# State-space mixer of a hybrid encoder: the pooling product as one float32 matmul, rows read back on GpSimd's queue, and another order of the work

## The chip, the cores and the metric

The kernel runs on one core of a Trainium2 chip. The metric is the device time of one execution in microseconds (us), as the median of the runs of one version. A profile of one execution stands beside it. The engines are TensorE (PE, with its weight loads as PEld), VectorE (DVE), ScalarE (ACT), GpSimd (POOL) and SyncE (SP); SP, ACT and POOL also issue transfers, each on a queue of its own.

## What is computed

The reference is a trunk of two layers on 512 tokens of 1024 channels: a SwiGLU feed-forward part, a mixer, and a second feed-forward part in each. The change touches the mixer of the first layer, whose 1024 projected channels go half to a pooling mixer and half to a state-space mixer:

```
z  = hn @ ab_w_in
ya = pool_mixer(z[..., :512])      # 4 groups of 128 channels, windows 2, 4, 8, 16
yb = s5_mixer(z[..., 512:])        # 32 groups of 16 channels, 64 complex states each
m  = concatenate([ya, yb]) @ ab_w_out

# pool_mixer, group gi, window w:
p = windowed_mean(u, w) - u        # the mean over the tokens that lie inside the sequence
y = (p @ w_grp[gi]) * scale
# s5_mixer: s_t = lambda * s_(t-1) + B u_t, forward and backward; y = C s + D u
y = gelu(y);  y = y * sigmoid(y @ w_glu + b_glu)
```

## The kernel before

Most products are made from float32 operands as three matmuls on rounded parts (`mm3`, L179): each operand is a high part (`hi`, rounded on ACT) and a low part (`lo`, the rest, on DVE). Weights pass through the class `Weights` (`self.W`): `_load` issues a tile of 512 KB on SP's queue into one of two raw buffers, `hi` and `lo` (L117, L128) split it, `fill(n)` splits up to n tiles ahead of those in use, `take` hands out a split tile, `done` gives one back and by default fills again; a new load can't be issued before the low part of the tile in its raw buffer is made. Each engine and each queue works in the order of the program; an instruction that waits holds up what stands behind it on its engine or queue.

The mixer (L1373) begins with `first_proj` (L362), the projection of the four state-space tiles in two halves of the tokens; between the halves `start` allocates its tiles and issues the first loads. `chunk_rows` writes each projected tile to memory (`z_dram`, ACT's queue), and `u_rows` reads two tiles back, re-cut by chunk of tokens, into `us` (SP's queue). The state-space part then runs for four channel tiles `ct`: `inject` (float32 matmuls of `us` with a table `m` into the one tile `ps_x`), `decay` (a tile `rho` of decay factors on ACT), `scan` (on DVE: two products from `ps_x` with a table `e`, which release it, a sum and a difference, four recurrences, two products, four half-height sums; it is a generator that stops after the first two products and after the recurrences), `permute` (two copies of a table `i` on ACT), `output` (float32 matmuls with `us`, the states and a table `g` into `ps_y`, then a Gelu on ACT and a write to `y_dram` on ACT's queue), `y_rows` (read back, SP) and `split_y` (parts of y).

The pooling part runs for four channel tiles `i`: `pool_tile` (projection of 24 matmuls into `ps_p`, two copies `pz` and `pp` on ACT, window sums, edge factors and a difference on GpSimd; the returned `rest` splits the result into the tiles `yhl`, ACT and DVE), and `pool_out` (three matmuls with `w_pool`, then hi on ACT and lo on DVE, L399 and L400, into the tiles `xh`, `xl`, which the projection read before). `out_a` (L1553) multiplies tiles `kt` of the result with the output weights `w_ao` into `psA`; three of its four accumulators lie in the three banks `ps_A`, which `pool_out` uses as well. `glu` is the gate product; it begins after `output(3)`. The order of all of this is written out by hand in L1563 to L1640.

Of the kernel before, what the change touches and what calls it, by code (L numbers as in the profile page):

```python
# [15 lines left out]
P = 128  # L16
# [157 lines left out]
class Builder:  # L174
# [1198 lines left out]
    def mixer(self, nxt, before):  # L1373
# [20 lines left out]
        def start():  # L1394
            nonlocal yp, y, yhl, sp, us, edge
            yp = tc.alloc_tile_pool(name="mix_y", bufs=1)
            y = yp.tile([P, 4, SEQ], F32, name="y")
            yhl = [yp.tile([P, 4, SEQ], F32R, name=n) for n in ("y_hi", "y_lo")]
            sp = tc.alloc_tile_pool(name="mix", bufs=1)
            edge = sp.tile([P, 4, 16], F32, name="edge")  # L1400
            G.dma_start(edge, ins["pool_edge"].partition_broadcast(P))
            us = sp.tile([P, 32, 64], F32, name="us")
            load("m0", "e0")

        def chunk_rows(ct, ps):
# [5 lines left out]
            if ct == 2:  # L1411
                u_rows(0)

        def u_rows(ct):
            nc.sync.dma_start(us[:, 8 * ct:8 * ct + 16], self.by_chunk(self.z_dram[ct * P:(ct + 2) * P]))

        yp = y = yhl = sp = us = edge = None
        self.first_proj(4, "mix", before, start, chunk_rows)
        load("m1")
        u_rows(2)  # L1420
# [15 lines left out]
        def decay(ct):  # L1436
            rho = con[ct, "rho"] = sp.tile([P, 2, 4, 64], F32, tag="rho", bufs=2, name="rho")
# [65 lines left out]
        def split_y(ct):  # L1503
            hi, lo = (z[:, ct] for z in yhl)
# [3 lines left out]
        def pool_tile(i):  # L1508
# [23 lines left out]
            for k, (a, b) in enumerate(((0, win // 2), (SEQ - win // 2 + 1, SEQ))):  # L1532
                if b > a:
                    G.tensor_tensor(out=z[:, pad + a:pad + b], in0=z[:, pad + a:pad + b],
                                    in1=edge[:, i, 8 * k:8 * k + b - a], op=ALU.mult)
            G.tensor_tensor(out=p, in0=z[:, pad:pad + SEQ], in1=p, op=ALU.subtract)

            def rest():
                hl = [v[:, i] for v in yhl]
                nc.scalar.copy(hl[0], p)  # L1540
                V.tensor_tensor(out=hl[1], in0=p, in1=hl[0].bitcast(F32), op=ALU.subtract)

            return rest

        def pool_out(i):
            ps = self.bank("ps_A" if i < 3 else "ps_p")
            self.mm3(ps, [z[:, i * P:(i + 1) * P] for z in w_pool], [v[:, i] for v in yhl], True, True)
            self.split_evac(xh[:, i], xl[:, i], ps, scol[:, i:i + 1])

        lhs = lambda kt: (xh[:, kt], xl[:, kt])  # L1550
# [10 lines left out]
        for i, win in enumerate(self.POOL_W):  # L1561
            G.tensor_scalar(out=scol[:, i:i + 1], in0=scol[:, i:i + 1], scalar1=1.0 / win, scalar2=None, op0=ALU.mult)
        rest = [pool_tile(0)]  # L1563
        decay(0)
        decay(1)
        inject(0)
        load("g0")
        for _ in scan(0):
            pass
        rest.append(pool_tile(1))  # L1570
        rest[0]()
        decay(2)
        inject(1)
        load("m3", "e2")
        for _ in scan(1):
            pass
        rest.append(pool_tile(2))
        rest[1]()
        permute(0)
        decay(3)  # L1580
        inject(2)
        load("i1", "g1")
        self.W.done()
        output(0)
        turn = scan(2)
        next(turn)
        rest[2]()
        self.W.done()
        y_rows(0)
        load("e3", "g2")  # L1590
        for _ in turn:
            pass
        rest.append(pool_tile(3))
        permute(1)
        inject(3)
        output(1)
# [3 lines left out]
        w_pool = self.W.take()  # L1600
        for i in range(3):
            pool_out(i)
        turn = scan(3)
        next(turn)
        rest[3]()
        self.W.done()
        permute(2)
        out_a(range(3), range(2))
        next(turn)
        pool_out(3)  # L1610
        for _ in turn:
# [259 lines left out]
```

## Time and profile before

| | us |
|---|---|
| median of 3 runs | 1858.05 (1857.41 to 1858.77) |
| profiled execution, its own time | 1858.23 |
| its span, first to last instruction | 1856.5 |
| PE busy | 1796.5 |
| DVE busy | 1491.7 |
| ACT busy | 944.5 |
| POOL busy | 360.7 |

The mixer lies between 391 and 545 us of the span. A timeline row gives the start, the length, the engine, the line, the operation with output and inputs, the number of instructions merged into it, and in square brackets the idle time of the engine just ahead of it and what ended it. Matmuls overlap, so the pace of a run of them is read from start to start and not from their lengths. The granted clock (PEclk) is 1.00 at 2.4 GHz and 0.50 at 1.2 GHz.

### The profile page before, as it was taken

Reading aid. Unit: us, or ns where it says so; the run is one execution under the profiler, and the core shown is the slowest. Engines: PE = TensorE matmul, PEld = TensorE weight load, DVE = VectorE, ACT = ScalarE, POOL = GpSimd, SP = SyncE. Lnnn points to the kernel's source line nnn. Section 1 sums busy time; section 2 is a strip of 40 time slices with the busy share of each in tenths; the row PEclk is TensorE's granted clock in tenths of the full one; section 3 lists DMA queues with packets and bytes.
Section 4 is the critical chain, followed back from the end, with each engine's and each line's share of the span. In section 5 each row is a group of like instructions: output and inputs, shape, how many; then the busy total and the mean of one; then the engine's idle time right before and its main releaser. Section 6 shows DMA issues by size and latency. Waiting matters only on the chain.

```text
span 1856.5 us, 31301 instructions
## 1 busy us (share of the span) xinstructions
PE 1796.5 (97%) x12144; PEld 1623.3 (87%) x12144; DVE 1491.7 (80%) x2396; ACT 944.5 (51%) x1769; POOL 360.7 (19%) x254
## 2 busy tenths in 40 slices
PE   8999999998899999999999999999999999999998
PEld 7877997787679999988899998889888799999886
DVE  6898989968769999854899997456788689999745
ACT  6254456365455454444644545446777664454532
POOL 1021321014011323200123221001333013223100
PEclk9999999999999999999999999999999999999999
DMA  5474346637542333232233333223333223332331
GB/s 198 137 230 158 111 135 191 208 133 250 172 134 72 103 104 111 95 125 91 80 103 103 103 103 125 91 79 101 95 113 111 94 82 103 105 112 92 125 102 57
DMA packets 88931, 224.40 MB, mean 121 GB/s; under 512 B 16560, under 2 KB 29008, under 8 KB 87760
## 3 DMA queue, kind: packets, MB, share of 16 engines
q1 hardware_dynamic: 77088, 196.75, 32.5%
q0 software_dynamic: 6960, 23.57, 4.2%
q10 hardware_dynamic: 4736, 2.10, 0.4%
q8 instruction: 95, 1.56, 0.3%
q14 instruction: 52, 0.43, 0.1%
HBM read 205.64 MB, written 18.84 MB: 121 GB/s over the span
## 4 chain that ended last, share of the span: by engine, by line
PE 58%; DVE 9%; ACT 4%; issue 2%; DMA 1%; POOL 0%; DVEq 0%; ACTq 0%; POOLq 0%
PE ps_gu L183 10%; PE ps_gu L182 10%; PE ps_gu L181 10%; PE ps_A L181 3%; PE ps_A L183 3%; PE ps_A L182 3%; PE ps_B L183 3%; PE ps_B L182 3%; PE ps_B L181 3%; PE ps_f L181 2%; PE ps_f L183 2%; DVE w_lo L135 2%; PE ps_f L182 2%; ACT junk L237 1%; DVE xsum L518 1%
## 5 line engine op out<-in xcount | busy, mean ns | idle before, releaser
L135 DVE TENSOR_TENSOR w_lo<-w_raw,w_hi 128x1024 fp32r<-128x1024 f32 x214 | 283.0, 1327 | 210.7 <-ACT w_hi L124 208.0
L124 ACT CAST w_hi<-w_raw 128x1024 fp32r<-128x1024 f32 (+1 forms) x313 | 263.0, 864 | 280.3 <-PE ps_A L183 72.5
L183 PE MATMUL ps_gu<-xT_hi,w_lo 128*128 128x256 f32 (+1 forms) x1008 | 307.4, 305 | 2.5 <-DVE w_lo L135 2.5
L183 PE MATMUL ps_gu<-xsum,w_lo 128*128 128x256 f32 x1088 | 308.3, 283 | 0.8 <-DVE w_lo L135 0.8
L182 PE MATMUL ps_gu<-xsum,w_hi 128*128 128x256 f32 x1088 | 308.0, 283 | 0.2 <-DVE xsum L518 0.2
L181 PE MATMUL ps_gu<-xsum,w_hi 128*128 128x256 f32 x1088 | 307.7, 283 | 0.0
L181 PE MATMUL ps_gu<-xT_hi,w_hi 128*128 128x256 f32 (+1 forms) x1008 | 304.9, 302 | 0.0
L182 PE MATMUL ps_gu<-xT_lo,w_hi 128*128 128x256 f32 (+1 forms) x1008 | 304.6, 302 | 0.0
L183 PEld LDWEIGHTS ps_gu<-xsum,w_lo 128*128 128x128 f32 x1088 | 208.6, 192 | 1.0 <-DVE w_lo L135 0.9
L182 PEld LDWEIGHTS ps_gu<-xsum,w_hi 128*128 128x128 f32 x1088 | 208.5, 192 | 0.4 <-DVE xsum L518 0.4
L181 PEld LDWEIGHTS ps_gu<-xsum,w_hi 128*128 128x128 f32 x1088 | 208.4, 192 | 0.0
L183 PEld LDWEIGHTS ps_gu<-xT_hi,w_lo 128*128 128x128 f32 x1008 | 190.4, 189 | 14.8 <-DVE w_lo L135 3.9
L181 PEld LDWEIGHTS ps_gu<-xT_hi,w_hi 128*128 128x128 f32 x1008 | 190.3, 189 | 8.5 <-issue 0.9
L182 PEld LDWEIGHTS ps_gu<-xT_lo,w_hi 128*128 128x128 f32 x1008 | 190.2, 189 | 7.3
L109 POOL TENSOR_TENSOR w_u<-w_raw,w_s 128x512 f32<-128x512 f32 x64 | 112.1, 1751 | 355.2 <-ACT w_hi L124 196.1
L124 ACT CAST w_hi<-w_s 128x512 fp32r<-128x512 f32 x136 | 77.8, 622 | 197.4 <-DVE w_s L105 193.6
L135 POOL TENSOR_TENSOR w_lo<-w_raw,w_hi 128x1024 fp32r<-128x1024 f32 x31 | 74.2, 2394 | 494.9 <-ACT w_hi L124 471.2
L105 DVE TENSOR_TENSOR w_s<-w_raw,w_u 128x1024 f32<-128x1024 f32 x68 | 145.8, 2144 | 2.3
L640 POOL TENSOR_TENSOR g<-g,m 128x1024 f32<-128x1024 f32 x34 | 94.5, 2780 | 245.0 <-DVE m L638 245.0
L181 PE MATMUL ps_B<-w_hi,gT 128*128 128x512 f32 x352 | 137.1, 389 | 1.7 <-DVE free L1302 1.7
L183 PE MATMUL ps_A<-w_hi,gT 128*128 128x512 f32 x352 | 137.1, 389 | 1.1 <-DVE gT L693 1.1
L181 PE MATMUL ps_A<-w_hi,gT 128*128 128x512 f32 x352 | 137.3, 390 | 0.0
(381 smaller groups left out, 4229.5 us busy)
## 6 DMA issues: line engine op xcount, KB each, us to landing
w_raw<-in_w_gu_dram SPq DMA_DIRECT2D x106, 512.0 KB, 3.4
w_raw<-in_w_dn_dram SPq DMA_DIRECT2D x88, 512.0 KB, 3.3
w_u<-in_w_gu_dram SPq DMA_DIRECT2D x70, 512.0 KB, 3.8
w_raw<-in_w_qk_dram SPq DMA_DIRECT2D x16, 512.0 KB, 3.4
w_raw<-in_w_in_dram SPq DMA_DIRECT2D x8, 512.0 KB, 3.3
cm<-m_dram SPq DMA_DIRECT2D x4, 1024.0 KB, 9.3
w_raw<-in_w_ao_dram SPq DMA_DIRECT2D x8, 512.0 KB, 4.2
cg<-g_dram SPq DMA_DIRECT2D x4, 1024.0 KB, 8.0
```

The lines of the kernel that those rows point to most:

```text
L105: tt(out=blocks(s), in0=g[:, :HALF].unsqueeze(1).broadcast_to([P, 2, HALF]), in1=blocks(u)[:, :2], op=ALU.subtract)
L109: (h_engine or self.nc.gpsimd).tensor_tensor(out=z["h"], in0=g[:, HALF:], in1=z["s"][:, HALF:], op=ALU.add)
L124: self.nc.scalar.copy(hi[:, k:k + step], src[:, k:k + step])
L135: (engine or self.lo_engine).tensor_tensor(out=lo[:, :n], in0=src, in1=hi[:, :n].bitcast(F32), op=ALU.subtract)
L181: mm(ps, a[0], b[0], start=start, stop=False)
L182: mm(ps, a[0], b[1], start=False, stop=False)
L183: mm(ps, a[1], b[0], start=False, stop=stop)
L237: self.nc.scalar.activation(out=junk[:, :src.shape[-1]], in_=src, func=AF.Square, scale=scale, accum_out=out)
L518: tt(out=forms[n][1], in0=x, in1=forms[n][0].bitcast(F32), op=ALU.subtract)
L640: nc.gpsimd.tensor_tensor(out=rows(f), in0=rows(f), in1=m, op=ALU.mult)
```

## The change

The pool product becomes one float32 matmul on the unsplit result and unsplit weights; `w_pool` is no longer a tile of the weight list but is loaded by itself on GpSimd's queue (256 KB), so the splits of the four pooled results and of `w_pool` go. The results of the pool product go to the tiles `yhl`, under a new name, and no longer to `xh` and `xl`; the parts of y go to `xh` and `xl` in their place. So a pool product need not wait for the last pooling projection, and the four stand apart in the new order, each with its low part put off to a later point (`run_lows`). Each projected tile is read back into `us` on GpSimd's queue as soon as it is written, instead of two at a time on SP's. The load of `m1` moves into `start`. `rho` has one buffer instead of two. The edge factors of both ends are applied in one instruction, and the scales are multiplied in one. The order of the mixer's work is written anew: `inject` and `pool_tile` change places, `decay` stands beside its own scan, and the splits of the two `w_ao` tiles stand behind scan 1 and behind scan 2. The diff, without the constants of the edge table and the weight list, from which `w_pool` is taken out:

```diff
@@ -1392,15 +1392,17 @@
                                   src if kind == "e" else src.rearrange("p u x -> p (u x)"))
 
         def start():
-            nonlocal yp, y, yhl, sp, us, edge
+            nonlocal yp, y, yhl, sp, us, edge, w_pool
             yp = tc.alloc_tile_pool(name="mix_y", bufs=1)
             y = yp.tile([P, 4, SEQ], F32, name="y")
-            yhl = [yp.tile([P, 4, SEQ], F32R, name=n) for n in ("y_hi", "y_lo")]
+            yhl = [yp.tile([P, 4, SEQ], F32R, name=n) for n in ("pool_hi", "pool_lo")]
             sp = tc.alloc_tile_pool(name="mix", bufs=1)
-            edge = sp.tile([P, 4, 16], F32, name="edge")
+            edge = sp.tile([P, 4, 17], F32, name="edge")
             G.dma_start(edge, ins["pool_edge"].partition_broadcast(P))
+            w_pool = sp.tile([P, HALF], F32, name="w_pool")
+            G.dma_start(w_pool, ins["w_pool"])
             us = sp.tile([P, 32, 64], F32, name="us")
-            load("m0", "e0")
+            load("m0", "e0", "m1")
 
         def chunk_rows(ct, ps):
 
@@ -1408,16 +1410,10 @@
             nc.scalar.copy(zt, ps)
             rows = self.z_dram[ct * P:(ct + 1) * P]
             nc.scalar.dma_start(rows, zt)
-            if ct == 2:
-                u_rows(0)
-
-        def u_rows(ct):
-            nc.sync.dma_start(us[:, 8 * ct:8 * ct + 16], self.by_chunk(self.z_dram[ct * P:(ct + 2) * P]))
-
-        yp = y = yhl = sp = us = edge = None
+            G.dma_start(us[:, 8 * ct:8 * ct + 8], self.by_chunk(rows))
+
+        yp = y = yhl = sp = us = edge = w_pool = None
         self.first_proj(4, "mix", before, start, chunk_rows)
-        load("m1")
-        u_rows(2)
         load("m2", "e1", "i0")
         self.new_psum(ps_x=(1, 1024), ps_y=2, ps_p=1, ps_A=3)
 
@@ -1434,7 +1430,7 @@
                                              us[:, 8 * ct + 2 * n + a, :], start=True, stop=True)
 
         def decay(ct):
-            rho = con[ct, "rho"] = sp.tile([P, 2, 4, 64], F32, tag="rho", bufs=2, name="rho")
+            rho = con[ct, "rho"] = sp.tile([P, 2, 4, 64], F32, tag="rho", bufs=1, name="rho")
             for d in range(2):
                 col = 16 * d + 4 * ct
                 nc.scalar.copy(rho[:, d], self.rho8[:, col:col + 4].unsqueeze(2).broadcast_to([P, 4, 64]))
@@ -1501,7 +1497,7 @@
             nc.sync.dma_start(y[:, ct], self.y_dram[ct * P:(ct + 1) * P])
 
         def split_y(ct):
-            hi, lo = (z[:, ct] for z in yhl)
+            hi, lo = xh[:, ct], xl[:, ct]
             nc.scalar.copy(hi, y[:, ct])
             V.tensor_tensor(out=lo, in0=y[:, ct], in1=hi.bitcast(F32), op=ALU.subtract)
 
@@ -1529,25 +1525,18 @@
                     G.tensor_tensor(out=s[:, o + h:e - h], in0=z[:, o:e - 2 * h], in1=z[:, o + 2 * h:e], op=ALU.add)
                     o, e = o + h, e - h
                 z, s = s, z
-            for k, (a, b) in enumerate(((0, win // 2), (SEQ - win // 2 + 1, SEQ))):
-                if b > a:
-                    G.tensor_tensor(out=z[:, pad + a:pad + b], in0=z[:, pad + a:pad + b],
-                                    in1=edge[:, i, 8 * k:8 * k + b - a], op=ALU.mult)
+            ends = z[:, pad:pad + SEQ].rearrange("p (a n) -> p a n", n=8)[:, 0:64:63]
+            G.tensor_tensor(out=ends, in0=ends, in1=edge[:, i, :16].rearrange("p (a n) -> p a n", n=8), op=ALU.mult)
             G.tensor_tensor(out=p, in0=z[:, pad:pad + SEQ], in1=p, op=ALU.subtract)
-
-            def rest():
-                hl = [v[:, i] for v in yhl]
-                nc.scalar.copy(hl[0], p)
-                V.tensor_tensor(out=hl[1], in0=p, in1=hl[0].bitcast(F32), op=ALU.subtract)
-
-            return rest
-
-        def pool_out(i):
+            pooled.append(p)
+
+        def pool_out(i, later):
+
             ps = self.bank("ps_A" if i < 3 else "ps_p")
-            self.mm3(ps, [z[:, i * P:(i + 1) * P] for z in w_pool], [v[:, i] for v in yhl], True, True)
-            self.split_evac(xh[:, i], xl[:, i], ps, scol[:, i:i + 1])
-
-        lhs = lambda kt: (xh[:, kt], xl[:, kt])
+            nc.tensor.matmul(ps, w_pool[:, i * P:(i + 1) * P], pooled[i], start=True, stop=True)
+            self.split_evac(*(x[:, i] for x in yhl), ps, scol[:, i:i + 1], later)
+
+        lhs = lambda kt: [x[:, kt] for x in (yhl if kt < 4 else (xh, xl))]
         psA, wA = [None] * TT, []
 
         def out_a(ts, kts):
@@ -1558,65 +1547,73 @@
                     psA[t] = self.bank("ps_A" if t < 3 else "ps_y")
                 self.rows(psA[t], lhs, kt, t, wA[kt // 2], kt % 2, kt == 0, kt == KT - 1)
 
-        for i, win in enumerate(self.POOL_W):
-            G.tensor_scalar(out=scol[:, i:i + 1], in0=scol[:, i:i + 1], scalar1=1.0 / win, scalar2=None, op0=ALU.mult)
-        rest = [pool_tile(0)]
+        pooled, lows = [], []
+
+        def run_lows():
+            while lows:
+                lows.pop(0)()
+
+        G.tensor_tensor(out=scol, in0=scol, in1=edge[:, :, 16], op=ALU.mult)
         decay(0)
-        decay(1)
         inject(0)
+        pool_tile(0)
         load("g0")
         for _ in scan(0):
             pass
-        rest.append(pool_tile(1))
-        rest[0]()
+        decay(1)
+        inject(1)
+        pool_tile(1)
+        load("m3", "e2")
+        turn = scan(1)
+        next(turn)
+        permute(0)
+        inject(2)
+        pool_out(0, lows)
+        for _ in turn:
+            pass
+        run_lows()
+        self.W.done(2, fill=False)
+        self.W.fill(3)
         decay(2)
-        inject(1)
-        load("m3", "e2")
-        for _ in scan(1):
-            pass
-        rest.append(pool_tile(2))
-        rest[1]()
-        permute(0)
-        decay(3)
-        inject(2)
         load("i1", "g1")
-        self.W.done()
+        pool_tile(2)
         output(0)
+        y_rows(0)
+        load("e3", "g2")
         turn = scan(2)
         next(turn)
-        rest[2]()
-        self.W.done()
-        y_rows(0)
-        load("e3", "g2")
+        inject(3)
+        pool_out(1, lows)
+        pool_tile(3)
+        self.W.done(2, fill=False)
+        permute(1)
+        output(1)
         for _ in turn:
             pass
-        rest.append(pool_tile(3))
-        permute(1)
-        inject(3)
-        output(1)
+        run_lows()
+        self.W.fill(2)
+        decay(3)
         load("i2")
         y_rows(1)
         load("g3", "i3")
-        w_pool = self.W.take()
-        for i in range(3):
-            pool_out(i)
+        pool_out(2, lows)
+        out_a(range(3), range(2))
         turn = scan(3)
         next(turn)
-        rest[3]()
-        self.W.done()
+        run_lows()
         permute(2)
-        out_a(range(3), range(2))
+        pool_out(3, lows)
+        output(2)
         next(turn)
-        pool_out(3)
+        run_lows()
+        out_a(range(3), range(2, 4))
         for _ in turn:
             pass
-        output(2)
         permute(3)
         split_y(0)
         split_y(1)
-        out_a(range(3), range(2, 4))
         y_rows(2)
-        self.W.done(2)
+        self.W.fill(4)
         output(3)
         y_rows(3)
         wide = self.bank("ps_x")
...
```

## Rows read from the trace of the kernel before

**Rows 1.** The page: busy time of each engine, share of the span, instructions.

```profile
PE 1796.5 (97%) x12144; PEld 1623.3 (87%) x12144; DVE 1491.7 (80%) x2396; ACT 944.5 (51%) x1769; POOL 360.7 (19%) x254
```

**Rows 2.** Windows: length, busy time by engine, granted clock, DMA share, GB/s.

```profile
424.00:475.00 51.00, 36.57 (x535) 30.73 (x534) 47.54 (x50) 26.67 (x43) 22.95 (x27) 0.93 0.74 249
475.00:505.00 30.00, 29.94 (x288) 24.14 (x287) 20.73 (x26) 12.36 (x16) 0.00 (x0) 0.95 0.54 167
```

**Rows 3.** Timeline of TensorE in the mixer.

```profile
426.87 0.50 PE L181 MATMUL ps_p<-xT_hi,w_hi 128*128 128x512 f32 x1
...
432.66 2.09 PE L1432 MATMUL ps_x<-us,cm 128*64 128x64 f32 x64
...
444.01 3.53 PE L1432 MATMUL ps_x<-us,cm 128*64 128x64 f32 x64 [3.19 <-issue]
...
459.39 2.09 PE L1432 MATMUL ps_x<-us,cm 128*64 128x64 f32 x64 [3.25 <-issue]
461.28 0.32 PE L1489 MATMUL ps_y<-us,perm 128*64 128x64 f32 x4
...
474.23 0.80 PE L181 MATMUL ps_A<-w_hi,xT_hi 128*128 128x512 f32 x1 [7.66 <-DVE xT_lo L400]
...
478.12 0.39 PE L181 MATMUL ps_A<-w_hi,xT_hi 128*128 128x512 f32 x1
...
483.94 0.50 PE L181 MATMUL ps_A<-w_hi,xT_hi 128*128 128x512 f32 x1
...
488.33 0.34 PE L1489 MATMUL ps_y<-us,perm 128*64 128x64 f32 x4
...
491.52 0.50 PE L181 MATMUL ps_x<-y_hi,w_hi 128*128 128x512 f32 x1
```

**Rows 4.** Timeline of VectorE in the mixer.

```profile
422.00 1.22 DVE L135 TENSOR_TENSOR w_lo<-w_raw,w_hi 128x1024 fp32r<-128x1024 f32 x1 [1.62 <-ACT w_hi L124]
426.79 1.22 DVE L1450 TENSOR_TENSOR t<-ps_x,ce 128x1024 f32<-128x1024 f32 x1 [3.57 <-PE ps_x L1432]
...
436.30 4.62 DVE L1467 TENSOR_TENSOR s<-t,t 64x512 f32<-64x512 f32 x4
...
475.40 1.21 DVE L1450 TENSOR_TENSOR t<-ps_x,ce 128x1024 f32<-128x1024 f32 x1
...
486.18 2.81 DVE L1467 TENSOR_TENSOR s<-t,t 64x512 f32<-64x512 f32 x4
```

**Rows 5.** The tile pp's instructions: count, ns min/median/max, first and last start.

```profile
L1541 DVE TENSOR_TENSOR y_lo<-pp,y_hi x4: 682/694/1008, 440.9 to 477.7; 128x512 fp32r<-128x512 f32 x4
```

**Rows 6.** Timeline of ScalarE in the mixer (ACTq is its transfers).

```profile
411.21 0.35 ACTq L1410 DMA_DIRECT2D z_dram<-zt  x1
...
420.92 1.05 ACT L124 CAST w_hi<-w_raw 128x1024 fp32r<-128x1024 f32 x1 [1.16 <-DMA w_raw<-in_w_in_dram]
...
456.17 1.09 ACT L1519 COPY pz<-ps_p 128x512 f32<-128x512 f32 x1 [0.26 <-PE ps_p L183]
...
457.98 2.10 ACT L1476 COPY perm<-ci 128x512 f32<-128x512 f32 x2
464.37 0.60 ACT L1496 ACTIVATE yt<-ps_y 128x512 f32<-128x512 f32 x1 [4.29 <-PE ps_y L1493]
```

**Rows 7.** Transfers, KB, us to landing (unnamed row: reads into us); last: GpSimd issues.

```profile
z_dram<-zt ACTq DMA_DIRECT2D x1, 256.0 KB, 3.2
...
DMA to landing us min/median/max: 5.9/7.6/9.2
...
ci<-i_dram SPq DMA_DIRECT2D x1, 512.0 KB, 4.1
...
g_dram<-ssm_tab POOLq DMA_DIRECT2D x10, 256.0 KB, 3.5
...
L1284 POOL DMA_DIRECT2D g_dram<-ssm_tab x10 | 7.6, 769 | 27.9 <-ACT ssm_tab L1279 27.9
```

**Rows 8.** Windows, columns as in rows 2: the stretch behind the 3.19 us stand.

```profile
444.00:446.00 2.00, 1.99 (x38) 2.00 (x40) 2.00 (x2) 1.35 (x2) 1.84 (x3) 0.50 0.37 150
```

More of the change, by code (lines that the diff above doesn't have):

```diff
@@ L1630, in glu @@
                 self.mm3(psG[d], [z[:, kt % 2 * HALF + d * P:kt % 2 * HALF + (d + 1) * P] for z in wG[kt // 2]],
-                         [z[:, kt] for z in yhl], kt == 0, kt == 3)
+                         [z[:, kt] for z in (xh, xl)], kt == 0, kt == 3)
         glu(range(3), range(2))
@@ L1684, in mid_weights @@
         if ly == 0:
-            l = [w["w_in"][i] for i in (4, 5, 6, 7, 0, 1, 2, 3)] + [w["w_pool"]]
+            l = [w["w_in"][i] for i in (4, 5, 6, 7, 0, 1, 2, 3)]
             l += [w["w_ao"][0, i] for i in range(2)] + [w["w_glu"][i] for i in range(2)]
@@ L1816, in lay_out @@
     bias = bias.reshape(16, 4, P, 256).transpose(0, 2, 1, 3)
-    edge = np.zeros((4, 16), np.float32)
+    edge = np.ones((4, 17), np.float32)
     for i, w in enumerate(Builder.POOL_W):
         edge[i, :w // 2] = [w / (t + w // 2) for t in range(w // 2)]
-        edge[i, 8:7 + w // 2] = [w / (w - 1 - k) for k in range(w // 2 - 1)]
+        edge[i, 17 - w // 2:16] = [w / (w - 1 - k) for k in range(w // 2 - 1)]
+        edge[i, 16] = 1 / w
     lanes = lambda z: z.reshape(2, 16, 2, 64, -1).transpose(2, 3, 0, 1, 4).reshape(P, 32, -1)
@@ L1838, in lay_out @@
         "w_in": col_tiles(a["ab_w_in"][0]),
-        "w_pool": np.concatenate([a["pool_w"][0].transpose(1, 0, 2).reshape(P, HALF),
-                                  np.zeros((P, HALF), np.float32)], axis=1),
+        "w_pool": a["pool_w"][0].transpose(1, 0, 2).reshape(P, HALF),
         "w_glu": a["ssm_w_glu"][0].reshape(2, 2, P, HALF).transpose(0, 2, 1, 3).reshape(2, P, 1024),
```

## The prediction

> **What bounds the kernel now.** I read the shares of busy time first: TensorE (PE) is busy 97% of the span [rows 1], so nothing can be won where PE never waits. The busy times by stretch then show where it does wait: from 424 to 475 us, inside the state-space mixer, PE is busy 36.57 of 51 us and VectorE (DVE) 47.54, while from 475 to 505 PE is busy 29.94 of 30 [rows 2]. The change works in just that first stretch. PE's own order of work shows the three stands: 3.19 us before inject(2), 3.25 before inject(3), 7.66 before the output product out_a [rows 3]. The first two wait for a scan's first two products (L1450, L1451), which release the one `ps_x` tile; the third waits for the low part of a pooled result (L400), which stands on DVE behind scan 2. So DVE's queue is the pace: from its first scan product at 426.79, which sat idle 3.57 us before, to the end of scan 3 at 486.18+2.81 = 488.99 [rows 4]. PE then ends output(3) and begins the gate product at 491.52 [rows 3]. Behind that point the code is unchanged, so I compare the start of the gate product, and every microsecond there counts as one in the total. The profiled execution took 1858.23 (span 1856.5 and 1.7 around it), the median of the runs 1858.05; I apply the difference to the median.
>
> **Work that goes.** Four splits of pooled results: on DVE 0.69, once 1.01, in sum 3.1 us [rows 5], and as many copies on ScalarE (ACT). One weight split (`w_pool`): about 1.2 on DVE and 1.05 on ACT [rows 4, 6]. With GpSimd out of the way the pieces overlap a little, so DVE's queue gets some 3.9 us shorter. GpSimd does four edge products instead of seven and one scaling instead of four; it only has to be done by the time a pool product wants its tile, and that is later than its work in all of what follows.
>
> **The product.** Three rounded matmuls of about 0.23 (18 of them take 488.33-483.94 = 4.4) make 0.70; the float32 one is not in the trace at 512 columns. inject is float32: 32 matmuls of 64 columns in 2.09 us [rows 3]. If the two 64-wide halves run one after the other, 512 columns cost 8 x 2.09/32 = 0.52; if side by side, 1.04. I take 0.9, nearer the second, since the halves use different columns of the array. Four of them: between -0.7 and +1.4 us of PE, I take +0.8, of which only the last stands on the path below (+0.2, bounds -0.2 and +0.3). The Trainium skill (FP8 and Floating Point Precision, TensorE Precision Notes) says that true float32 makes four passes, which speaks against the change, as an estimate 4/3 of 0.70 = 0.93 and the same sum within 0.1.
>
> **The start.** Scan 0 needs inject(0), and that the rows `us` of its chunk. Before, a pair of chunks came back on SyncE's queue; now each one on GpSimd's. The first row write is issued at 411.21 [rows 6] and landed 3.2 later; a GpSimd issue of this kind takes 0.77, and 256 KB on its queue landed in 3.5, while the `us` reads took 5.9 to 9.2 [rows 7]. So us(0) lands between 418.7 and 424.4; I take 420.3, near the first, since it has half the bytes. inject(0) adds 2.0 (459.39 to 461.28 [rows 3]): 422.3. But DVE first has the low part of the fourth `w_in` tile, which ended at 422.00+1.22 = 423.2, and its ACT half had waited 1.16 for the load [rows 4, 6]. Now `m1`, 1 MB, stands ahead of that load: at 249 GB/s [rows 2] at most 4.2 us, at least 0; it is issued when the second half of the projection begins, long before, so I take 1.2, near the lower end. Scan 0 begins at 424.4 (423.2 to 427.4), 2.4 us sooner. PE stands about 1.3 us at 419 and does pool_tile(0) later; the cover is its wait at inject(2), which stays.
>
> **The new order, step by step.** Between 426.79 and 488.99 DVE has four scans and, beside them, 3.1 of pool splits, 3.7 of three weight splits and 2.8 of pooled low parts: (62.2-9.6)/4 = 13.2 us a scan. Scans 0 and 1: 424.4+26.4 = 450.8. Low part of product 0 and the first `w_ao` split: 0.7+1.2, 452.7. First two products of scan 2: 2.4, 455.1; now `ps_x` is free. PE: inject(3) 2.0, product 1 0.9, pool_tile(3) 5.8 (426.87 to 432.66): 463.8. ACT: the copies `pz` and `pp` 1.8 (456.17 to 457.98) and the first of permute(1) 1.05: 466.7. output(1) to its Gelu 3.1 (461.28 to 464.37): 469.8. Gelu 0.6 and the issue of its write 0.35 [rows 6]: 470.8. Here is the new wait: the high part of the second `w_ao` tile stands behind this Gelu on ACT (`fill(2)` after output(1)), 1.05, 471.8, and DVE had finished scan 2 and product 1's low part at 455.1+10.8+0.7 = 466.6. It stands 5.2 us, which is most of the 6.3 (2.4+3.9) it had won. Behind that wait are queued on DVE the low part (1.2, 473.0), scan 3's first two products (2.4, 475.4) and the low part of product 2 (0.7, 476.1). For that last one PE waits: out_a's third token tile wants the third `ps_A` bank, which product 2 holds. PE's own work reached this at 469.8+0.9+1.5 = 472.2, so it stands 3.9 us. Then 12 of out_a's 18 matmuls 2.9, product 3 0.9, output(2) 3.0, the second out_a 4.4, output(3) with its end 3.2 (488.33 to 491.52): 490.5. That is 1.0 sooner than 491.5.
>
> **What lies beside.** `i2` is queued on SyncE behind the load that waits for that second low part: 473.0+0.4, landing 4.1 later [rows 7], 477.5; permute(2) ends at 479.6, product 3's high part at 480.5, its low part on DVE at 481.2, and scan 3's last part takes 5.2 (two products as long as its first two, 2.4, and sums of 2.81 [rows 4]): 486.4, inside PE's 487.3. `e3` stands behind y_rows(0), which waits for output(0)'s write. inject(2) waits for scan 1's first two products (437.6+2.4 = 440.0); with 3.5 for it as before, a product 0.9, pool_tile(2) 5.8, output(0) 3.1 and the Gelu the write is issued near 454.3: even with 9.2 for the write and for `e3` [rows 7] it lands at 472.7, as scan 3 begins. One `rho` buffer makes ACT wait for each scan's recurrences; behind them are queued the pool copies, which PE delivers later anyway.
>
> **The clock.** After the stand of 7.66 us the first nine matmuls took from 474.23 to 478.12, 3.9 us where nine of 0.23 are 2.1: 1.8 lost. After 3.19 us the granted clock was 0.50 (the 1.2 GHz level) and inject took 3.53; after 3.25 us it took 2.09 as ever [rows 3, 8]. The new stand of 3.9 us lies between: half of 1.8, +0.9. Sum: -1.0+0.9 = -0.1, 1858.1 against 1858.23, and 1858.0 by the median.
>
> **The rivals.** *Scans run free, faster.* Scan 3, beside an idle GpSimd, took 488.99-475.40 less 2.4 for others = 11.2, and four half-height sums beside GpSimd's adds took 4.62 instead of 2.81 [rows 4]. If the new order keeps GpSimd's adds away from scans 0 and 1 (2.0 each) and the start loses nothing to `m1` (1.2), all of the chain is 5.2 sooner: 1852.8. For it: DVE is the pace up to scan 2. Against: the same adds run, and two pool tiles still fall in those scans. By the Trainium skill (SBUF - State Buffer, Who interferes with whom) only VectorE instructions with two SBUF inputs contend with GpSimd's reads; the slow sums agree, and products with one PSUM input go free. By that, pool_tile(1)'s adds beside scan 1's first products would cost about 1 us less, 1857.0. Chance 0.27 for more than 3.7 us sooner.
>
> *A crowded start, slower.* `m1`, `w_pool`, the row writes and the small pieces of `us` on a third queue share the DMA engines; if all of `m1` (4.2) delays us(0) and its read takes 9.2, it lands at 414.4+4.2+0.8+9.2 = 428.6, scan 0 begins at 430.8, 6.4 later than I say: 1864.4. It decides from a scan start of 424.4 on, one for one, and is slower by over 0.2% from 428.2. Against: GpSimd's own queue landed such sizes in 3.5. Chance 0.15.
>
> *The edit doesn't act as read.* The third bank comes free otherwise, or the product costs 0.52: output(2) is then held by permute(2)'s first copy, 478.6, and the end is 1.3 sooner still, 0.9 more without the cold clock: 1855.8. That lies within 0.2%, with the forecast: together 0.58.
>
> **How the numbers follow.** 0.2% is 3.7 us, about what a measurement of this kernel can tell from no change. Faster 0.27, same 0.58, slower 0.15. The likeliest case alone reaches from 1854.3 to 1861.7. The range goes down to the free scans and up to the middle of the crowded start: 1852.5 to 1862.5.
>
> **What would show it.** Right: scan 0's first product near 424.4; DVE idle some 5 us before the second `w_ao` low part, released by ACT; PE idle some 4 us in out_a, released by L400; the stand of 7.66 gone; the gate product near 490 to 491.5. Wrong: DVE busy without a break up to scan 3 (then the gate product comes near 485), scan 0 after 427, or a wait for `e3` or `i2` that sets scan 3.

## The result: slower by 0.8%, and the profile after

The changed kernel takes 1873.62 us at the median (1868.87 to 1879.24), the kernel before 1858.77 beside it: a ratio of 1.0079 (1.0065 to 1.0094). The forecast was 1858.0 with a range up to 1862.5, so it was wrong, and on the side to which it gave a chance of 0.15. The profiled execution took 1873.31, 15.1 more than that of before.

The page, as [rows 1], and the windows, as [rows 2]. PE waits less than before in the first stretch (40.20 busy of 51, before 36.57), though part of that busy time is a lower granted clock (0.87, before 0.93), and more in the second (26.01 of 30, before 29.94), where it had no idle time to lose; the granted clock falls there from 0.95 to 0.83.

```profile
PE 1802.2 (96%) x12140; PEld 1626.1 (87%) x12140; DVE 1485.5 (79%) x2391; ACT 941.3 (50%) x1764; POOL 362.3 (19%) x253
...
424.00:475.00 51.00, 40.20 (x454) 32.96 (x454) 43.69 (x46) 18.38 (x30) 18.42 (x25) 0.87 0.61 215
475.00:505.00 30.00, 26.01 (x337) 20.99 (x338) 17.42 (x22) 13.95 (x20) 4.38 (x5) 0.83 0.40 128
```

TensorE's timeline, as [rows 3]: the stands are the numbers in brackets, with what ended them. inject(0) and inject(3) now follow stands of 4.65 and 6.08 us, output(1) one of 3.06. The last one, 3.61, lies behind the gate product, where no code was changed.

```profile
424.67 3.68 PE L1428 MATMUL ps_x<-us,cm 128*64 128x64 f32 x64 [4.65 <-issue]
...
461.85 3.41 PE L1428 MATMUL ps_x<-us,cm 128*64 128x64 f32 x64 [6.08 <-issue]
465.18 1.13 PE L1536 MATMUL ps_A<-pp,w_pool 128*128 128x512 f32 x2
465.74 0.80 PE L181 MATMUL ps_p<-xT_hi,w_hi 128*128 128x512 f32 x1
...
474.96 0.45 PE L1485 MATMUL ps_y<-us,perm 128*64 128x64 f32 x4 [3.06 <-ACT perm L1472]
...
485.96 0.80 PE L181 MATMUL ps_A<-w_hi,pool_hi 128*128 128x512 f32 x1 [3.99 <-DVE pool_lo L400]
...
491.25 1.45 PE L1536 MATMUL ps_p<-pp,w_pool 128*128 128x512 f32 x2
...
502.92 0.50 PE L181 MATMUL ps_x<-xT_hi,w_hi 128*128 128x512 f32 x1
...
532.93 0.39 PE L183 MATMUL ps_B<-w_hi,pool_lo 128*128 128x512 f32 x1
536.92 0.80 PE L181 MATMUL ps_B<-w_hi,pool_hi 128*128 128x512 f32 x1 [3.61 <-ACT junk L237]
```

VectorE's timeline, as [rows 4]: scan 0 begins at 428.39; in scan 1 the recurrences (L1455) take 4.39 and the four sums (L1463) 4.38, in scan 2 they take 2.43 and 2.79; then DVE stands 10.14 us for the high part of the second `w_ao` tile.

```profile
428.39 1.22 DVE L1446 TENSOR_TENSOR t<-ps_x,ce 128x1024 f32<-128x1024 f32 x1 [3.10 <-PE ps_x L1428]
...
441.63 1.23 DVE L1446 TENSOR_TENSOR t<-ps_x,ce 128x1024 f32<-128x1024 f32 x1
...
446.14 4.39 DVE L1455 TENSOR_TENSOR_SCAN t<-rho,t 128x256 f32<-128x256 f32 x4
...
453.08 4.38 DVE L1463 TENSOR_TENSOR s<-t,t 64x512 f32<-64x512 f32 x4
...
462.99 2.43 DVE L1455 TENSOR_TENSOR_SCAN t<-rho,t 128x256 f32<-128x256 f32 x4
...
468.05 2.79 DVE L1463 TENSOR_TENSOR s<-t,t 64x512 f32<-64x512 f32 x4
...
481.76 1.23 DVE L135 TENSOR_TENSOR w_lo<-w_raw,w_hi 128x1024 fp32r<-128x1024 f32 x1 [10.14 <-ACT w_hi L124]
```

GpSimd's additions for pool_tile(1) and pool_tile(2) both begin inside scan 1:

```profile
445.75 1.42 POOL L1525 TENSOR_TENSOR pz<-pz 128x541 f32<-128x541 f32 x1
...
455.49 2.90 POOL L1525 TENSOR_TENSOR pz<-pz 128x541 f32<-128x541 f32 x2
```

ScalarE's timeline, as [rows 6], says why VectorE stands those 10.14 us: the high part `w_hi` stands behind the Gelu of output(1), that behind permute(1), that behind the copies `pz` and `pp` of pool_tile(3).

```profile
471.99 1.07 ACT L1515 COPY pz<-ps_p 128x512 f32<-128x512 f32 x1 [4.96 <-PE ps_p L183]
472.86 1.13 ACT L1516 ACTIVATE pp<-ps_p 128x512 f32<-128x512 f32 x1
473.77 2.07 ACT L1472 COPY perm<-ci 128x512 f32<-128x512 f32 x2
479.63 0.60 ACT L1492 ACTIVATE yt<-ps_y 128x512 f32<-128x512 f32 x1 [3.78 <-PE ps_y L1489]
480.26 0.38 ACTq L1493 DMA_DIRECT2D y_dram<-yt  x1
480.68 1.05 ACT L124 CAST w_hi<-w_raw 128x1024 fp32r<-128x1024 f32 x1 [0.45 <-ACT yt L1492]
```

Transfers issued in one microsecond each (KB, us to landing), as [rows 7]: `m1` needs 10.4 us, and the first row write, issued behind it at 411.78, 8.2 where it was 3.2; the first read of `us`, issued at 420.25, needs 4.3 more.

```profile
cm<-m_dram SPq DMA_DIRECT2D x1, 1024.0 KB, 10.4
...
z_dram<-zt ACTq DMA_DIRECT2D x1, 256.0 KB, 8.2
...
us<-z_dram POOLq DMA_DIRECT2D x1, 256.0 KB, 4.3
```

### The profile page after: what moved, and what is told of

Same layout as the page of the kernel before. It is cut to its first block, busy times and chain, and to the rows that moved or that the text cites. A ratio compares the mean times of both kernels' runs of the same rounds, so it can differ in the third digit from the quotient of the medians.

```text
span 1871.5 us, 31290 instructions
## 1 busy us (share of the span) xinstructions
PE 1802.2 (96%) x12140; PEld 1626.1 (87%) x12140; DVE 1485.5 (79%) x2391; ACT 941.3 (50%) x1764; POOL 362.3 (19%) x253
## 3 DMA queue, kind: packets, MB, share of 16 engines
q8 instruction: 95, 1.56, 0.4%
## 4 chain that ended last, share of the span: by engine, by line
PE 64%; DVE 17%; ACT 6%; DMA 6%; issue 4%; POOL 1%; SPq 1%; DVEq 0%; ACTq 0%; POOLq 0%
PE ps_gu L183 11%; PE ps_gu L182 11%; PE ps_gu L181 11%; DVE w_lo L135 3%; PE ps_A L181 3%; PE ps_A L182 3%; PE ps_A L183 3%; PE ps_B L181 3%; PE ps_B L182 3%; PE ps_B L183 3%; DMA w_raw<-in_w_gu_dram 2%; ACT w_hi L124 2%; PE ps_f L183 2%; PE ps_f L181 2%; PE ps_f L182 2%
```

## The experiments

The code ahead of the mixer is the same in all kernels, yet `m0`'s load is issued between 404.68 and 410.07 us of the span in their profiled executions. So beside the median of the timed runs the table has the traces' times counted from that issue (start of the named instruction, for scans 1 and 3 the end of the last sum, for the column "end" the end of the span). Each of those times is of one execution. The kernel before, run again beside each group of experiments, took 1857.92 to 1859.28 at the median.

| kernel | scan 0 | scan 1 ends | inject(3) | scan 3 begins | scan 3 ends | gate product | second tile of ps_B | end | median, us |
|---|---|---|---|---|---|---|---|---|---|
| before | 19.78 | 48.15 | 52.38 | 68.39 | 81.97 | 84.50 | 115.05 | 1449.4 | 1858.77 |
| changed | 20.81 | 49.87 | 54.26 | 75.32 | 91.93 | 95.33 | 129.34 | 1464.0 | 1873.62 |
| e2_m1_late | 18.37 | 46.45 | 50.85 | 72.81 | 88.05 | 91.46 | 125.36 | 1460.4 | 1867.34 |
| e3_hi_early | 20.68 | 48.69 | 53.09 | 64.04 | 84.92 | 88.31 | 122.27 | 1457.0 | 1867.27 |
| e5_bank_order | 20.51 | 49.57 | 53.96 | 74.81 | 91.24 | 94.64 | 125.25 | 1458.5 | 1870.15 |
| e6_three | 18.04 | 45.03 | 49.83 | 62.53 | 82.51 | 85.92 | 116.13 | 1448.9 | 1857.12 |
| e7_three_perm | 17.29 | 45.08 | 49.36 | 63.05 | 78.41 | 81.83 | 112.17 | 1445.3 | 1854.23 |
| e8_us_sp | 22.72 | 50.15 | 54.54 | 75.44 | 91.88 | 95.29 | 129.24 | 1463.1 | 1871.25 |
| e10_before_f32b | 20.10 | 48.45 | 52.07 | 67.65 | 80.70 | 84.05 | 114.38 | 1445.9 | 1856.84 |
| e12_perm_us_sp | 20.15 | 49.15 | 53.54 | 64.35 | 81.48 | 84.90 | 115.15 | 1448.7 | 1859.47 |
| e13_no_adds | 20.51 | 45.41 | 49.69 | 69.43 | 86.03 | 89.45 | 123.42 | 1457.3 | 1866.94 |
| e14_before_no_adds | 20.09 | 45.60 | 49.83 | 63.01 | 76.58 | 79.11 | 109.35 | 1442.4 | 1852.04 |
| e15_warm | 19.07 | 46.90 | 52.04 | 71.60 | 88.07 | 91.47 | 121.72 | 1455.5 | 1863.63 |

My theory was three separate losses: a crowded start, the place of one ScalarE instruction, and one PSUM bank. The rivals stand in each expectation.

**The start.** e2 puts `m1` back behind the first projection.

```
-            load("m0", "e0", "m1")
+            load("m0", "e0")
...
-        load("m2", "e1", "i0")
+        load("m1", "m2", "e1", "i0")
```

> The changed kernel with m1 loaded behind the first projection again, as in the kernel before; the small reads of us stay on GpSimd's queue and w_pool stays early. Theory (crowded start): without this 1 MB the first row write lands 3 to 5 us after its issue instead of 8.2, us(0) is there near 420.5, scan 0 starts near 424.5 instead of 428.4, and the cold stand before inject(0) is gone: 3 to 5 us less, about 1869.6. Rival (the reads on GpSimd's queue or w_pool are what is slow): us(0) still lands near 424 and the time stays at 1873.6.

The first row write, issued at 408.88, landed in 4.3 us instead of 8.2, scan 0 began 2.4 us sooner by the table, the end came 3.6 sooner, the median fell by 6.3. (The two profiled executions differ by 6.5, of which 2.9 lie ahead of `m0`, so the table's 3.6 is the better measure; 1.0 of it is a shorter scan 1.) So `m1` was in the way, as the rival "crowded start" had it.

```profile
z_dram<-zt ACTq DMA_DIRECT2D x1, 256.0 KB, 4.3
```

e4 makes the same edit the other way round, in the kernel before: `load("m0", "e0", "m1")`, and no `load("m1")` behind.

> The kernel before with one edit of the change, m1 loaded with m0 ahead of the second half of the first projection. Theory (crowded start): its row writes land late as in the changed kernel, scan 0 starts 2 to 4 us later than 426.8, the time rises by 2 to 4 us, to about 1861.5. Rival (the crowd comes from w_pool or from the small reads): no change, 1858.8.

It took 1857.91, no change: here the rival held. The first row write did land late (6.8 us), but a pair of chunks waits for the second write anyway, and that landed at 420.02 instead of 418.43; inject(0) began 0.3 us later, counted from `m0`. So an early `m1` costs only the one who reads each chunk as soon as it is written: it takes back what the single reads should win. e8 undoes those in the changed kernel, where `m1` stays early:

```
-            G.dma_start(us[:, 8 * ct:8 * ct + 8], self.by_chunk(rows))
+            if ct % 2:
+                ct -= 1
+                nc.sync.dma_start(us[:, 8 * ct:8 * ct + 16], self.by_chunk(self.z_dram[ct * P:(ct + 2) * P]))
```

The read now stands behind the second row write, where the kernel before has it behind the third, so on SyncE's queue the last `w_in` load comes after it; inject(0) waits for `us` all the same (5.70 us in e8, 3.46 in e12).

> The changed kernel with one part undone: the rows us come back on SyncE's queue, two chunks at a time, as in the kernel before; m1 stays early. Theory: beside an early m1 the first row write lands late and the four small reads win nothing, as m1 early cost the kernel before nothing: scan 0 starts within 1 us of 428.4 and the time stays within 2 us of 1873.6. Rival (the reads are slow because GpSimd's queue carries them): scan 0 starts 2 to 4 us sooner and the time falls by as much, to about 1870.5.

Scan 0 came 1.9 later, more than the 1 us I allowed, and the median was 1871.25, 2.4 lower and a little outside the 2 us too; 0.9 of that the kernel before was lower as well. By the table the gate product came at the same time (95.29, 95.33), since scan 1 then took 14.3 us (35.86 to 50.15) instead of 15.9; the 0.8 by which the end came sooner arose behind the gate product. The rival's sooner scan 0 did not come. With `m1` out of the way the single reads are worth their place, as e12 shows (e7 below, with the edit of e8):

> As e7_three_perm (m1 late), with us read on SyncE's queue in pairs of chunks. Theory: with no m1 in the way the single reads do win; without them us(0) lands some 2.5 us later and scan 0 starts as much later: 1 to 3 us more than e7_three_perm, about 1856. Rival (single reads on GpSimd's queue are worth nothing in any order): 1854.2.

Scan 0 began 2.9 us later than in e7, the end came 3.4 later, the median 5.2: the theory, and more than its 3 us. The Trainium skill (DMA: Bandwidth & Descriptors, Issuing engines are not separate DMA queues) says that transfers started by different engines run on the same 16 DMA engines and interleave. By that the third queue gave the row writes and the reads no lane of their own; the 8.2 against 4.3 us agrees.

**ScalarE's order.** e3 puts one call, the high part of the second `w_ao` tile, ahead of pool_tile(3).

```
         pool_out(1, lows)
+        self.W.hi()
         pool_tile(3)
```

> The changed kernel with ScalarE's high part of the second w_ao tile put ahead of pool_tile(3), so behind no Gelu. Theory: VectorE's stand of 10.1 us before the second w_ao low part is gone or under 2 us, scan 3 starts some 9 us sooner, TensorE's stand of 4.0 us in out_a and the cold clock behind it go: 4 to 6 us less, about 1868.5. Rival (TensorE is the pace by then: output(1) and what it waits for set the end): VectorE's stand moves to another wait and the time changes by less than 1.5 us.

VectorE's stand is gone, as ScalarE's and VectorE's timelines of e3 show: the high part is made at 465.37, the low part follows scan 2 at 468.91, and scan 3 begins 11.3 us sooner by the table.

```profile
465.37 1.04 ACT L124 CAST w_hi<-w_raw 128x1024 fp32r<-128x1024 f32 x1
...
468.91 1.22 DVE L135 TENSOR_TENSOR w_lo<-w_raw,w_hi 128x1024 fp32r<-128x1024 f32 x1
470.05 1.22 DVE L1446 TENSOR_TENSOR t<-ps_x,ce 128x1024 f32<-128x1024 f32 x1
...
479.38 0.75 DVE L400 SCALAR_TENSOR_TENSOR pool_lo<-ps_A,mix_scol,pool_hi 128x512 fp32r<-128x512 f32 x1 [6.98 <-ACT pool_hi L399]
```

The gate product came 7.0 sooner, the median fell by 6.4. What is late next stands in the last row: product 2, which on TensorE is queued behind output(1), and output(1) behind permute(1).

**The bank.** Each accumulator of out_a and of `ps_B` in this program lies in a PSUM bank of its own. Behind the gate product TensorE stood 3.61 us, released by ScalarE's last read of the fourth out_a tile (`ps_y`). In the order of the changed kernel TensorE uses its accumulators in another order first, and with it they get other banks. The numbers of the banks are the program's, no trace shows them: there the second tile of `ps_B` lies on bank 7 in both kernels; before, that was the second out_a tile's, after, the fourth's, which is read last. e1 exchanged two names:

```
+        psB[1], psB[2] = psB[2], psB[1]
```

> The changed kernel with the second and third accumulators of its second output half exchanged, nothing else. Theory: the stand of 3.6 us ahead of the second token tile there, and the half clock behind it (1.4 us), come only from the PSUM bank that this accumulator falls on (bank 7, still read by the last tile of the first half). On bank 6 it starts at once: the stand is gone, 5 us less, about 1868.6. Rival: the second half is late for its operands or its weights, and the wait moves to the next matmul: no change, 1873.6.

It took 1875.36, with the same stand, 3.52 us: banks go by first use, so the exchange left them as they were. It told nothing of the theory but how banks are given out. e5 exchanged two groups of products, so that the fourth out_a tile comes first and gets bank 6:

```
-        glu((3,), range(2))
         out_a((3,), range(2))
+        glu((3,), range(2))
```

> The changed kernel with two neighbouring groups of TensorE's work exchanged (first products of the fourth out_a tile ahead of those of the fourth gate tile), so that the last out_a tile falls on PSUM bank 6 and the gate tile on bank 7. The exchange of the accumulators' names in e1_bank left the banks as they were, so the bank theory is still untested. Theory: the second token tile of the second output half (bank 7) then follows a gate tile that was read long before; the stand of 3.6 us and the half clock behind it are gone, 5 us less, about 1869. Rival: another operand holds it: no change, 1874.

The second tile starts behind the first without a stand and at full pace (0.23 us from start to start):

```profile
534.62 0.40 PE L181 MATMUL ps_B<-w_hi,pool_hi 128*128 128x512 f32 x1
534.85 0.39 PE L182 MATMUL ps_B<-w_lo,pool_hi 128*128 128x512 f32 x1
535.08 0.40 PE L183 MATMUL ps_B<-w_hi,pool_lo 128*128 128x512 f32 x1
535.32 0.39 PE L181 MATMUL ps_B<-w_hi,pool_hi 128*128 128x512 f32 x1
```

From the gate product to this tile it is 30.6 us, as before (30.55), and not 34.0; the end came 5.5 sooner, the median fell by 3.5. 0.7 of the 5.5 lies ahead of the gate product, where the edit changed nothing, so the bank is worth 4.8. In e15 below, whose idle matmuls take two more accumulators ahead of it, the stand is gone as well (30.25 us).

**All three together**, e6 (e2, e3 and e5 in one):

> The changed kernel with three edits together: m1 loaded late, the high part of the second w_ao tile ahead of pool_tile(3), the bank exchange. Theory (three separate losses at three places): the gains add, 6 + 6 + 5 us, about 1857. Rival (the start and the stand of VectorE are the same slack counted twice): only some 6 + 5, about 1862.5.

1857.12: the gains add. By the table they were 3.6, 6.9 and 5.5 alone, in sum 16.0, and 15.0 together. So the three are separate, as far as single traces tell: the rival's 1862.5 is 5 us away. e7 goes on with what was late next:

```
+        load("i1", "g1")
         self.W.done(2, fill=False)
         self.W.fill(3)
         decay(2)
-        load("i1", "g1")
...
         self.W.hi()
+        permute(1)
         pool_tile(3)
         self.W.done(2, fill=False)
-        permute(1)
```

> As e6_three, and permute(1) ahead of pool_tile(3), with i1 and g1 issued ahead of the weight load that waits for VectorE. Theory: TensorE's stand of 3.1 us before output(1) and ScalarE's place behind pool_tile(3) go, product 2 and scan 3 come some 3 us sooner: 2 to 3 us under e6_three, about 1854.5. Rival (scan 3 waits for TensorE's other work): same as e6_three within 1 us.

1854.23, 2.9 under e6 and a ratio of 0.9974 (0.9963 to 0.9984) to the kernel before: faster than both kernels, than the kernel before by 0.26%. Its own largest stand is one that the late `m1` makes:

```profile
436.15 3.25 PE L1428 MATMUL ps_x<-us,cm 128*64 128x64 f32 x64 [5.48 <-DMA cm<-m_dram]
```

e11 issues `m1` between the two, behind the second row write (`if ct == 1: load("m1")` at the end of chunk_rows).

> As e7_three_perm, with m1 issued behind the second row write instead of behind the whole first projection. In e7_three_perm m1 lands at 436.0 and TensorE stands 5.5 us before inject(1). Theory: m1 lands near 430, that stand and the cold clock behind it go, and us(0) is already under way: 1 to 3 us less than e7_three_perm, about 1852.5. Rival (m1 crowds the later reads of us, or VectorE was no later for that stand): no gain, 1854.2.

1854.84, no gain: the stand before inject(1) was gone, but us(0) took 6.9 us instead of 5.3 to land and scan 0 began 2.0 us later (19.33 from `m0`). The rival held.

**VectorE beside GpSimd.** e10 does one part of the change alone, in the old order: the float32 product on rows that are not split. (Its first form, e9, was this with y_rows(1) in the old place; the second pooled tile was overwritten before its product, and TensorE stood 11.1 us for that transfer. Its 1864.46 says nothing of the product.)

```
-                nc.scalar.copy(hl[0], p)
-                V.tensor_tensor(out=hl[1], in0=p, in1=hl[0].bitcast(F32), op=ALU.subtract)
...
-            self.mm3(ps, [z[:, i * P:(i + 1) * P] for z in w_pool], [v[:, i] for v in yhl], True, True)
+            nc.tensor.matmul(ps, w_pool[:, i * P:(i + 1) * P], pooled[i], start=True, stop=True)
```

> The kernel before with one part of the change alone: the pooling product as one float32 matmul on pooled rows that are not split (they and w_pool lie in the y tile, which is free until then); order, us reads and loads as before. Theory (VectorE's queue is the pace of the kernel before): four splits of 0.7 and one weight split of 1.2 leave VectorE, the scans end some 3 us sooner and the time falls by 2 to 4, to about 1855.5. Rival (the float32 product costs TensorE more than this, or the scans' end is not the pace): within 1 us of 1858.4.

> As e9_before_f32, with y_rows(1) and the loads of g3 and i3 behind the three pool products: in e9_before_f32 the second pooled tile was overwritten by y's rows ahead of its product, which so waited for that transfer, and its time says nothing of the product. Theory (VectorE is the pace of the kernel before): 2 to 4 us less than 1858.6, about 1855.5. Rival (the scans' end is not what sets the end, or the product costs it): within 1 us of 1858.6.

1856.84 against 1857.92, a ratio of 0.999 (0.9981 to 0.9999): nearer the rival. The four splits, 3.1 us and 2.75 from start to start, are gone from VectorE, yet scan 3 ends only 1.3 sooner. Scan 0 began 0.3 later, and VectorE's timeline shows where the rest went: with the splits out of the way the sums and differences of scans 1 and 2 meet GpSimd's additions. In scan 1 they take 1.58 and 1.56 instead of 0.69 each, 0.6 more than the kernel before paid there; in scan 2, 1.56 and 1.80, and 0.5 is lost.

```profile
441.75 1.21 DVE L1453 TENSOR_TENSOR t<-ps_x,ce 128x1024 f32<-128x1024 f32 x1
443.00 1.58 DVE L1455 TENSOR_TENSOR t<-t,t 128x512 f32<-128x512 f32 x1
444.50 1.56 DVE L1456 TENSOR_TENSOR t<-t,t 128x512 f32<-128x512 f32 x1
...
459.88 1.56 DVE L1455 TENSOR_TENSOR t<-t,t 128x512 f32<-128x512 f32 x1
461.37 1.80 DVE L1456 TENSOR_TENSOR t<-t,t 128x512 f32<-128x512 f32 x1
```

Its TensorE rows also time the product, two of them in the first row and the third in the second:

```profile
463.23 1.99 PE L1544 MATMUL ps_A<-y 128*128 128x512 f32 x4
465.05 1.02 PE L1544 MATMUL ps_A<-pp,y 128*128 128x512 f32 x2
```

e13 and e14 leave GpSimd's window additions out (`for step in range(0)`), of the changed kernel and of the kernel before.

> The changed kernel without GpSimd's window additions (the pooled values are then not window sums; their edge products and subtractions stay). Theory: the additions slow VectorE's two-operand products, sums and recurrences beside them; without them scan 1 takes 12 to 13.5 us instead of 15.8, inject(3) and all behind it come 2 to 3 us sooner: about 1871. Rival (scan 1 is slow because of something else, its wait for inject(1)'s tile or its operands): scan 1 stays near 15.8 and the time at 1873.6.

> The kernel before without GpSimd's window additions (the pooled values are then not window sums). Theory: VectorE's chain of four scans, 62.2 us in the kernel before, loses some 5 us, the gate product comes 3 to 5 us sooner: about 1854.5. Rival (VectorE is no slower beside GpSimd than alone): no change, 1858.4.

1866.94 and 1852.04: 6.7 less in both, more than I had expected of either (about 1871 and 1854.5). Scan 1 of the changed kernel took 12.5 us instead of 15.9, inside the 12 to 13.5 of the theory, and the rows of e13's VectorE that answer to those above read 3.47 (beside the subtraction that stays on GpSimd) and 2.78:

```profile
445.02 3.47 DVE L1455 TENSOR_TENSOR_SCAN t<-rho,t 128x256 f32<-128x256 f32 x4
...
451.05 2.78 DVE L1463 TENSOR_TENSOR s<-t,t 64x512 f32<-64x512 f32 x4
```

Only instructions with both inputs in SBUF grew; the first products, with one input in PSUM, took 1.21 to 1.23 in every kernel. That is the rule that the forecast named from the Trainium skill (SBUF — State Buffer, Who interferes with whom), and these rows bear it out. (The page names VectorE's modes with two ports as a second case, beside the forecast's "only"; these rows don't show it.)

**The clock.** e15 fills the stands ahead of inject(0) and inject(3) with matmuls on `xT_hi` whose result nobody reads.

```
+        warm(18)
         inject(0)
...
+        warm(24)
         inject(3)
```

> The changed kernel with 18 idle matmuls ahead of inject(0) and 24 ahead of inject(3), which fill TensorE's stands there (they write an accumulator that nobody reads); by their place they also change the banks, so that the stand in the second output half goes as in e5_bank_order. Theory: kept busy, TensorE takes inject(0) in 2.1 us instead of 3.7 and inject(3) in 2.0 instead of 3.4, and the gate product comes 2 to 3 us sooner than in e5_bank_order: about 1867.5. Rival (the low clock has another cause than the stand, or the gain is lost in the next wait): as e5_bank_order, 1870.2.

```profile
419.49 4.24 PE L1435 MATMUL ps_y<-xT_hi 128*128 128x512 f32 x18
424.16 2.08 PE L1428 MATMUL ps_x<-us,cm 128*64 128x64 f32 x64 [0.43 <-issue]
...
453.60 5.73 PE L1435 MATMUL ps_y<-xT_hi 128*128 128x512 f32 x24
459.26 2.09 PE L1428 MATMUL ps_x<-us,cm 128*64 128x64 f32 x64
```

Both injects are back at 2.1 us, and the gate product came 3.2 sooner than in e5, the end 3.0. 1.2 of the 3.2 is a shorter scan 1 (14.7 instead of 15.9), which met GpSimd's additions elsewhere. The median, 1863.63, is 6.5 under e5's; of the 5.8 between the two profiled executions 2.85 lie ahead of `m0` (407.22 against 410.07), so they are no part of the edit.

## Why the prediction was wrong, step by step

| step | forecast | measured | late by |
|---|---|---|---|
| scan 0, first product | 424.4 | 428.39 | 4.0 |
| scan 1 ends | 450.8 | 457.46 | 6.7 |
| inject(3) begins | 455.1 | 461.85 | 6.8 |
| Gelu of output(1) | 469.8 | 479.63 | 9.8 |
| second `w_ao` low part | 471.8 | 481.76 | 10.0 |
| out_a goes on | 476.1 | 485.96 | 9.9 |
| gate product, clock in it | 491.4 | 502.92 | 11.5 |
| whole | 1858.1 | 1873.31 | 15.2 |

**The start: the mechanism was seen, but `m1` was charged to the wrong transfer.** Of us(0) I had written 418.7 to 424.4 and took 420.3; it was there at 424.58, beyond the upper end. I let the row write land in its old 3.2 us, with `m1` queued ahead of it, and charged `m1` only to the weight load, with 1.2 us. Measured, the write took 8.2 and the loads of `w_in` 6.4 and 4.9. Then inject(0) ran at a granted clock of 0.50 (1.2 GHz) and took 3.7 us, not 2.0. So scan 0 began at 428.39, just past the 428.2 from which I had called the rival decided; 0.57 of that was there ahead of `m0`. The rival's 1864.4 for 430.8 (its own terms give 430.6) was still too low, since it let the rest go as forecast. Before, pool_tile(0) filled TensorE's wait for us(0), and inject(0) began at 424.66 without a stand; in the new order TensorE stood 4.65 us there. To put pool_tile(0) back ahead of inject(0) was not tried.

**13.2 us a scan.** That was a mean over four scans of before, some beside GpSimd's additions and the last without. Scan 0 took 13.1, scan 1 15.9: the new order puts pool_tile(1)'s and pool_tile(2)'s additions both into it. The rival "scans run free" had looked at the same rows with the other sign. e13 shows that the additions are the cause. The same mistake stands behind the 3.9 us by which DVE's queue should get shorter: in e10, without the four splits, it was 1.6 from scan 0's first product to scan 3's end.

**The wait on ScalarE: right in its place, its releaser and what comes next, wrong in size.** DVE stood for the second `w_ao` high part behind output(1)'s Gelu, as said, but 10.14 us and not 5.2. Both sides moved: DVE was there 5 us later than forecast (471.6 against 466.6), the Gelu 9.8. Between inject(3) and that Gelu it lost 3.0 more, to inject(3) (3.41 instead of 2.0) and to output(1) behind its own stand of 3.06. PE's stand in out_a was 3.99, released by L400, where 3.9 stood in the text; the old stand of 7.66 is gone, as forecast.

**The clock, +0.9.** One stand was counted. There were five of 3 us and more, and behind each the granted clock was lower (columns as in [rows 2]; before, it was 1.00 in all of these stretches but 474 to 480, where it was 0.67):

```profile
424.00:430.00 6.00, 5.33 (x68) 4.96 (x69) 2.83 (x3) 1.06 (x5) 1.76 (x5) 0.50 1.00 311
458.00:464.00 6.00, 2.15 (x40) 2.19 (x42) 5.96 (x8) 0.00 (x0) 2.84 (x5) 0.50 0.77 200
474.00:480.00 6.00, 5.04 (x98) 4.74 (x99) 0.00 (x0) 2.22 (x3) 5.30 (x6) 0.72 0.01 3
485.00:492.00 7.00, 6.04 (x13) 4.46 (x14) 4.46 (x8) 2.08 (x2) 0.00 (x0) 0.52 0.97 365
536.00:540.00 4.00, 3.08 (x8) 2.46 (x8) 1.91 (x3) 2.67 (x4) 0.00 (x0) 0.57 0.41 135
```

The counted one alone, the 3.99 in out_a, cost 2.4 and not 0.9: the twelve matmuls behind it took 5.29 us (485.96 to 491.25) instead of 2.9, and product 3 then 1.38 (to 492.63) instead of 0.9. Less the 0.9 and a little that output(3) ran sooner, these are the 1.7 by which the last part was late. e15 shows that keeping PE busy in two of the others gives back up to 3.2 us at the gate product, the shorter scan 1 included. What the remaining ones cost by themselves was not tried.

**The product: right.** In e10 two of them took 1.82 us from start to start (463.23 to 465.05), 0.91 each, against the 0.9 that I took between 0.52 and 1.04. The estimate of 0.93 that the forecast made from the Trainium skill (FP8 and Floating Point Precision, TensorE Precision Notes) agrees with it.

**"Behind that point the code is unchanged, so every microsecond there counts as one in the total."** This was false, and no rival had it. The code was the same, but not where its accumulators lie: 3.61 us of stand and some 1.4 at the lower clock, which e5 took away.

The slips add up: 4.0 at the start, 2.7 in scan 1, 0.1 up to inject(3), 3.0 from there to the Gelu and 1.7 up to the gate product are the 11.5; the bank is 5; from there to the end the changed kernel made up about 1.

## What to carry to other kernels

A large load that is put ahead of a chain of a small write and a read lengthens what is under way beside it: here the write (8.2 instead of 4.3) and a weight load (6.4 instead of 4.4), not the read that came after `m1` had landed (4.3). Charge the new load to every transfer beside it, or move it behind the chain (e2: 3.6 us). When an order is rewritten, list for each engine what stands behind the instruction that waits longest; one ScalarE copy moved past a Gelu was worth 7 us (e3). Unchanged code behind a change still moves if its buffers do: look up which bank each accumulator gets, and who reads that bank last (e5).

## What the runs showed of the chip that I had not expected

Without GpSimd's window additions the whole kernel is 6.7 us faster, in either order (e13, e14), and VectorE's chain from scan 0's first product to scan 3's end is shorter by 5.6 and 5.7. That price doesn't go away when VectorE's work gets less: 3.1 us of splits taken off VectorE shortened the chain by 1.6 (e10), as other instructions with two SBUF inputs moved into the additions' time and stretched from 0.69 to 1.56.

Idle matmuls in a stand made the next ones faster: inject(0) 2.08 instead of 3.7 us, inject(3) 2.09 instead of 3.41, with 18 and 24 products in front (e15). A stand of 1.59 us (e7, before inject(0)) left the pace at 2.08, one of 5.48 gave 3.25.

The first row write, 256 KB, landed in 3.2 us in the kernel before, in 4.3 with `w_pool` loaded beside it (e2), in 6.8 with `m1` ahead (e4) and in 8.2 with both.
